# Expert MLP on one core: the first x tile loaded in two halves with different packet sizes, and the b2 load moved behind the entry of the main block

## The chip, the cores and the metric

The kernel runs on one core of one Trainium2 chip. The metric is the device time of one execution in microseconds. The core has a matrix engine (PE, whose weight loads are listed apart as PEld), a vector engine (DVE), a scalar engine (ACT), a general engine (POOL, written `nc.gpsimd` in the code) and a synchronising engine (SP, `nc.sync`). Sixteen DMA engines carry all transfers between the main memory and the core's on-chip memory. Loads that POOL issues run on the queue that the profile calls q0 (software_dynamic), those that SP issues on q1 (hardware_dynamic).

## What is computed

There are 8 experts. Each has 256 tokens, a hidden size of 512 and an inner size of 2048. All arrays arrive as 32-bit floats.

```python
h = np.maximum(np.matmul(x, w1) + b1[:, np.newaxis, :], 0)   # x 8x256x512, w1 8x512x2048
out = np.matmul(h, w2) + b2[:, np.newaxis, :]                # w2 8x2048x512
```

The weights are 8 x 4 MiB for `w1` and as much for `w2`; x and the output have 4 MiB each.

## The kernel before, in words

**Layers.** The inner size is cut into `nJ` = 16 columns of 128. For one expert, layer 1 (L288) makes 64 matmuls: 16 columns by 4 slices of the hidden size. The weights `w1sb` are the stationary operand and the turned input `xTsb` streams past them. ACT applies bias and relu to each column (L106) and writes `hTsb` in 16 bits. Layer 2 starts with the bias `b2` as a one-row matmul (L303) and adds 32 matmuls (L318), two token blocks by 16. ACT, and for the last two experts also DVE, carry the results out of the accumulators (L118). One loop on PE (L268) runs E + LAG = 11 steps: layer 1 of expert `step`, and from step 3 on layer 2 of expert `step - 3`.

**Loads of weights.** POOL issues them all (`run_gpsimd`, L157). `w1sb` and `w2sb` have three slots each. The load also converts from 32 to 16 bits, so a 4 MiB expert becomes 2048 KB. The order on q0 is written out by hand: `w1` of experts 0, 1 and 2 as early as possible, then, in step 3, `w1` of expert 3, `w2` of expert 0; x of experts 4 to 7 in step 4, and so on in turn. `w1` of expert e from 3 on waits until layer 1 of expert e - 3 is done (L162); `w2` waits in the same way for layer 2 (L167). At the end POOL and SP issue the output transfers (L187, L155, L389).

**The beginning, outside the main block.** `first_loads` (L340) issues on SP, in this order: x of expert 0 into `pair0`, x of expert 1 into `pair1` (512 KB each, 128 rows of 4 KB), the `b1` rows (64 KB), and x of experts 2 and 3 into `outg` (1024 KB, 128 rows of 8 KB). On POOL it issues `w1` of expert 0 and `b2` (8 KB when converted). `first_turns` (L354) builds an identity matrix (POOL zeroes `steps`, DVE turns it at L360, ACT copies four blocks at L363), casts x of experts 0 and 1 (ACT, L365), turns them with 16 matmuls against the identity (PE, L372), copies the result to `xTsb` (ACT, L373), and turns the `b1` rows with four DVE transposes (L375). The order of the instructions of these two functions on each engine is chosen by a scheduler, except for loads that `keep_in_program_order` fixes.

**The entry.** The rest runs inside a block (L381) whose order and semaphores are written by hand. ACT, DVE, PE and SP enter it only after everything ahead of it that it depends on is done: every load of `first_loads` has landed, and all of `first_turns` has run. POOL alone enters at once, issues `w1` of experts 1 and 2, and makes up for the wait later (L180). Within the block ACT first casts x of experts 2 and 3 (L195), and DVE turns it (L222).

**Semaphores near the change.** The arrival of `w1` of expert e counts on `s_w1[e % 3]`, 16 per load. SP waits for it at L144 and raises `w1_in`, for which PE waits (L271). Slot 1 is used by experts 1, 4 and 7.

Of the kernel before, what the change touches and what calls it, by code (L numbers as in the profile page):

```python
# [10 lines left out]
def kernel(  # L11
# [9 lines left out]
    nc = tc.nc  # L21
# [3 lines left out]
    E, T, H = x.shape  # L25
    M = w1.shape[2]
    P = 128
# [4 lines left out]
    nB = P // B  # L32
    LAG = 3
    NW = 3
# [13 lines left out]
    def sb(name, shape, dt=fp16):  # L48
        return nc.alloc_sbuf_tensor(name, shape, dt).ap()

    w1_f = sb("w1sb", [P, NW * nKC * M + nJ])
    w1_sb = w1_f[:, 0 : NW * nKC * M].rearrange("p (n kc m) -> p n kc m", n=NW, kc=nKC)
# [6 lines left out]
    b2_sb = sb("b2sb", [1, E * H])  # L59
    b1_rows = sb("b1rows", [E * nB, M // nB], fp32)  # L60
# [9 lines left out]
    def sem(name):  # L70
        return nc.alloc_semaphore(name)

    s_x = sem("s_x")
    s_w1 = [sem(f"s_w1_{i}") for i in range(NW)]
# [51 lines left out]
    def out_of(first, n):  # L126
        return out[first : first + n].rearrange("e (p r) h -> (e p) r h", r=n * nTB)

    x32 = {e: pair[e] for e in range(2)}
    x32[2] = grouped[0][:, 0 : FIRST[2] * nTB, :]  # L130

    def w1_of(e):
        return w1[e].rearrange("(p kc) m -> p kc m", kc=nKC)

    def x_of(first):
        n = FIRST[first]
        return x[first : first + n].rearrange("e (p r) h -> (e p) r h", r=n * nTB)

    def run_sync():
        s = nc.sync  # L140
        for step in range(E + LAG):
            if step < E:
                if step:
                    s.wait_ge(s_w1[step % NW], 16 * ((step + NW - 1) // NW))  # L144
                s.sem_inc(w1_in, 1)  # L145
            if step >= LAG:
                e = step - LAG
                for h in range(2):
                    if (e, h) in s_w2:
                        s.wait_ge(s_w2[e, h], 16)  # L150
                    s.sem_inc(w2_in, nQ // 2)  # L151
                    if e == E - 1 and h == 0:
                        s.wait_ge(po_free_a, E)
                        s.wait_ge(po_free_d, E)
                        s.dma_start(out=out_of(E - 2, 1), in_=pair[0]).then_inc(s_out[E - 2], 16)  # L155

    def run_gpsimd():  # L157
        g = nc.gpsimd

        def load_w1(e):  # L160
            if e >= NW:
                g.wait_ge(ph_full, nJ * (e - NW + 1))  # L162
            g.dma_start(out=w1_sb[:, e % NW], in_=w1_of(e)).then_inc(s_w1[e % NW], 16)  # L163

        def load_w2(e):
            if e >= NW:
                g.wait_ge(po_full, ENDS * (e - NW + 1))  # L167
            src = w2[e].rearrange("(p j) h -> p j h", j=nJ)
            cuts = (0, CUT[e], nJ) if e in CUT else (0, nJ)
            for h, (lo, hi) in enumerate(zip(cuts, cuts[1:])):  # L170
                g.dma_start(  # L171
                    out=w2_sb[:, e % NW, lo:hi], in_=src[:, lo:hi]).then_inc(s_w2[e, h], 16)

        for step in range(1, E + LAG):
            if step < E:
                if step == 4:
                    g.dma_start(out=x16[step], in_=x_of(step)).then_inc(s_x, 16)
                load_w1(step)
            if step == NW - 1:
                tc.wait_critical_data_deps()  # L180
            if step >= LAG:
                load_w2(step - LAG)
        g.wait_ge(s_w2[E - 1, 0], 16)
        for first in sorted(GROUPS, reverse=True):
            done = 1 + first + GROUPS[first]
            g.wait_ge(po_free_a, done)
            g.dma_start(out=out_of(first, GROUPS[first]), in_=grouped[first]).then_inc(  # L187
                s_out[first], 16)
# [149 lines left out]
                t.wait_ge(ph_free, turned)  # L338

    def first_loads():  # L340
        for to, rows in (
            (x32[0], x_of(0)),
            (x32[1], x_of(1)),
            (b1_rows, b1.rearrange("e (b i) -> (e b) i", b=nB)),
            (x32[2], x_of(2)),
        ):
            tc.keep_in_program_order(nc.sync.dma_start(out=to, in_=rows))  # L347
        for to, rows in (
            (w1_sb[:, 0], w1_of(0)),
            (b2_sb, b2.rearrange("e h -> (e h)").rearrange("(o f) -> o f", o=1)),  # L350
        ):
            tc.keep_in_program_order(nc.gpsimd.dma_start(out=to, in_=rows))

    def first_turns():  # L354
        g, v, a, t = nc.gpsimd, nc.vector, nc.scalar, nc.tensor
# [18 lines left out]
        for b in range(nB):  # L374
            v.transpose(  # L375
                out=b1T[b * B : (b + 1) * B, nB - 1 - b : nB - 1 - b + nJ * B],
                in_=b1_rows.rearrange("r (i j) -> r j i", j=nJ))

    first_loads()
    first_turns()  # L380
    with tc.tile_critical(sync_engine=mybir.EngineType.Pool, no_gpsimd_drain=True):  # L381
        run_gpsimd()
        run_sync()
        run_scalar()
        run_vector()
        run_tensor()
        nc.sync.wait_ge(po_free_a, 1 + E)
        nc.sync.wait_ge(po_free_d, 1 + E)
# [38 lines left out]
```

## Time and profile before

| | |
|---|---|
| median of three runs | 180.65 us (180.57 to 181.31) |
| the profiled execution's own time | 180.67 us |
| its span, first to last instruction | 178.9 us |
| mean granted TensorE clock | 0.969 |
| PE busy | 130.8 us, 73% of the span |
| ACT busy | 86.2 us, 48% |
| DVE busy | 37.7 us, 21% |
| POOL busy | 13.4 us, 7% |
| DMA packets and bytes | 3825 packets, 40.98 MB |
| share of the 16 DMA engines' span, q0 and q1 | 95.2% and 4.5% |

The span is measured by the hardware profiler from the first to the last instruction; the execution's own time has 1.8 us more around it. A row of the timeline gives start, duration, engine, line, operation and operands, and in brackets how long the engine sat idle before it and what ended that. The DMA view can be asked for any stretch of the span: it then counts the packets of each queue whose start falls into it, and a strip of 40 digits gives the busy share of the 16 engines in 40 equal slices of the stretch, in tenths. A row of its list of issues has the bytes of one load and the time from issue to landing.

The page counts 448 packets under 512 bytes and 28 loads and stores: 16 of these short packets to each, one for every DMA engine. They close a transfer and are called closing packets below.

### The profile page before, as it was taken

Reading aid. Unit: us, or ns where it says so; the run is one execution under the profiler, and the core shown is the slowest. Engines: PE = TensorE matmul, PEld = TensorE weight load, DVE = VectorE, ACT = ScalarE, POOL = GpSimd, SP = SyncE. Lnnn points to the kernel's source line nnn. Section 1 sums busy time; section 2 is a strip of 40 time slices with the busy share of each in tenths; the row PEclk is TensorE's granted clock in tenths of the full one; section 3 lists DMA queues with packets and bytes.
Section 4 is the critical chain, followed back from the end, with each engine's and each line's share of the span. In section 5 each row is a group of like instructions: output and inputs, shape, how many; then the busy total and the mean of one; then the engine's idle time right before and its main releaser. Section 6 shows DMA issues by size and latency. Waiting matters only on the chain.

```text
span 178.9 us, 2880 instructions
## 1 busy us (share of the span) xinstructions
PE 130.8 (73%) x800; PEld 87.1 (49%) x800; DVE 37.7 (21%) x39; ACT 86.2 (48%) x160; POOL 13.4 (7%) x30
## 2 busy tenths in 40 slices
PE   0002299596969996999949993899389997997950
PEld 0002178585858742794338642764178543442410
DVE  0074099500000299992000000000000000001010
ACT  3302847585877803892099408970578303131010
POOL 7100000302020001001000001000200002000200
PEclk9999999999999999699999999999969999999995
DMA  5999989999999999998999999999899899999996
GB/s 215 265 255 277 233 183 231 234 205 207 234 209 202 234 212 198 234 231 183 231 234 201 209 234 205 205 234 220 191 234 231 187 227 205 214 213 212 335 440 256
DMA packets 3825, 40.98 MB, mean 229 GB/s; under 512 B 448, under 2 KB 464, under 8 KB 1136
## 3 DMA queue, kind: packets, MB, share of 16 engines
q0 software_dynamic: 3056, 37.76, 95.2%
q1 hardware_dynamic: 768, 3.21, 4.5%
q14 instruction: 1, 0.01, 0.0%
HBM read 71.39 MB, written 4.19 MB: 422 GB/s over the span
## 4 chain that ended last, share of the span: by engine, by line
DMA 62%; PE 20%; DVE 6%; ACT 4%; issue 3%; SPq 1%; ACTq 0%
DMA w1sb<-in_w_dram 43%; PE ph L288 12%; DMA outg<-in_x_dram 10%; DMA w2sb<-in_w_dram 10%; PE po L318 8%; DVE xTsb L222 6%; ACT hTsb L106 3%; ACT x L195 1%; SPq L347 1%; PE po L303 0%; ACT pair L118 0%; ACTq L422 0%; SPq L145 0%; SPq L151 0%; ACTq L194 0%
## 5 line engine op out<-in xcount | busy, mean ns | idle before, releaser
L288 PE MATMUL ph<-xTsb,w1sb 128*128 x512 | 68.1, 293 | 21.7 <-SPq L145 10.4
L288 PEld LDWEIGHTS ph<-xTsb,w1sb 128*128 x512 | 59.0, 148 | 31.9 <-issue 29.0
L106 ACT ACTIVATE hTsb<-ph,b1T 128x256 f16<-128x256 f32 x128 | 56.8, 474 | 15.4 <-PE ph L288 14.9
L318 PE MATMUL po<-w2sb,hTsb 128*128 x256 | 56.6, 379 | 2.3 <-SPq L151 2.3
L118 ACT COPY outg<-po 32x1024 f32<-32x1024 f32 (+1 forms) x20 | 20.1, 1005 | 43.3 <-PE po L318 43.2
L318 PEld LDWEIGHTS po<-w2sb,hTsb 128*128 x256 | 25.0, 98 | 32.8 <-issue 5.0
L222 DVE STREAM_TRANSPOSE xTsb<-x 32x512 f16<-32x512 f16 (+1 forms) x32 | 31.0, 970 | 35.0 <-DMA x<-in_x_dram 27.7
L118 DVE COPY pair<-po 128x512 f32<-128x512 f32 x2 | 1.4, 691 | 88.4 <-PE po L318 88.4
L372 PE MATMUL ph<-ident,x 128*128 128x128 f16 x16 | 1.9, 313 | 16.6 <-ACT ident L363 16.6
L171 POOL DMA_DIRECT2D w2sb<-in_w_dram x10 | 5.3, 534 | 70.7 <-PE po L318 70.7
L372 PEld LDWEIGHTS <-x 128*128 128x128 f16 x16 | 1.6, 148 | 16.6 <-ACT ident L363 16.6
L163 POOL DMA_DIRECT2D w1sb<-in_w_dram x7 | 3.7, 535 | 64.6 <-PE ph L288 64.4
L118 ACT COPY pair<-po 128x512 f32<-128x512 f32 x2 | 1.2, 585 | 13.8 <-PE po L318 13.8
L375 DVE STREAM_TRANSPOSE b1T<-b1rows 32x512 f32<-32x512 f32 x4 | 4.1, 1023 | 10.2 <-DMA b1rows<-in_b_dram 10.1
L303 PE MATMUL po<-b2sb,ones 1*128 x16 | 4.8, 379 | 0.9 <-issue 0.7
L363 ACT COPY ident<-hTsb 32x32 f16<-32x32 f16 x4 | 1.0, 240 | 9.2 <-DVE hTsb L360 9.1
L365 ACT CAST x<-pair 128x1024 f16<-128x1024 f32 x2 | 2.1, 1044 | 2.3 <-DMA pair<-in_x_dram 2.3
L303 PEld LDWEIGHTS po<-b2sb,ones 1*128 1x128 f16 x16 | 1.4, 91 | 3.5 <-issue 3.3
L373 ACT COPY xTsb<-ph 128x1024 f16<-128x1024 f16 x2 | 1.9, 1015 | 1.1 <-PE ph L372 1.1
L187 POOL DMA_DIRECT2D out_dram<-outg x2 | 1.1, 536 | 16.7 <-DMA w2sb<-in_w_dram 16.7
L195 ACT CAST x<-outg 128x2048 f16<-128x2048 f32 x1 | 1.9, 1900 | 0.8 <-DMA outg<-in_x_dram 0.8
L365 ACT ACT_TABLE_LOAD x1 | 1.3, 1283 | 0.7 <-PEq L411 0.7
(12 smaller groups left out, 5.0 us busy)
## 6 DMA issues: line engine op xcount, KB each, us to landing
w1sb<-in_w_dram POOLq DMA_DIRECT2D x8, 2048.0 KB, 30.6
w2sb<-in_w_dram POOLq DMA_DIRECT2D x6, 2048.0 KB, 43.8
w2sb<-in_w_dram POOLq DMA_DIRECT2D x2, 1024.0 KB, 28.4
out_dram<-outg POOLq DMA_DIRECT2D x1, 2048.0 KB, 10.9
w2sb<-in_w_dram POOLq DMA_DIRECT2D x1, 1408.0 KB, 17.5
pair<-in_x_dram SPq DMA_DIRECT2D x2, 512.0 KB, 3.8
outg<-in_x_dram SPq DMA_DIRECT2D x1, 1024.0 KB, 17.8
x<-in_x_dram POOLq DMA_DIRECT2D x1, 1024.0 KB, 27.7
```

Of the source, the lines that this page charges most:

```text
L106: return nc.scalar.activation(out=to, in_=columns, func=relu_of, bias=b1T[:, at : at + 1], scale=1.0)
L118: return copy(out=t.rearrange("p (tb s) h -> p tb s h", s=split)[at : at + rows, lo:hi, k, :], in_=po[k * rows : (k + 1) * rows, e % 2, lo ...
L163: g.dma_start(out=w1_sb[:, e % NW], in_=w1_of(e)).then_inc(s_w1[e % NW], 16)
L171: g.dma_start(out=w2_sb[:, e % NW, lo:hi], in_=src[:, lo:hi]).then_inc(s_w2[e, h], 16)
L195: a.copy(out=x16[2], in_=x32[2]).then_inc(cast, 1)
L222: ins = v.transpose(out=to[b * B : (b + 1) * B, :, :, half * B : (half + 1) * B], in_=src.rearrange("p r (i kc) -> p kc r i", kc=nKC))
L288: ins = t.matmul(out=ph[i][:, 0:T], lhsT=w1_cols(w1_j, i, kc), rhs=x_cols[kc], start=(kc == 0), stop=(kc == nKC - 1),)
L303: t.matmul(out=po_f[:, bass.ds(o + tb * 512, H)], lhsT=ones1, rhs=b2_sb[0:1, bass.ds(b_e, H)], start=True, stop=False, skip_group_check=True,)
L318: ins = t.matmul(out=po_f[:, bass.ds(o + tb * 512, H)], lhsT=hT_f[:, bass.ds(h_e + (j * T + tb * P), P)], rhs=w2_f[:, bass.ds(w_e + j * H, ...
L365: a.copy(out=x16[e], in_=x32[e])
L372: t.transpose(out=to[:, kc, r, :], in_=rows[:, kc, :], identity=ident)
L375: v.transpose(out=b1T[b * B : (b + 1) * B, nB - 1 - b : nB - 1 - b + nJ * B], in_=b1_rows.rearrange("r (i j) -> r j i", j=nJ))
```

## The change

Three things are edited.

1. x of expert 0 is loaded by two instructions in place of one: partitions 0 to 63 cut into packets of 2 KB (`max_dma_last_dim` of 4 * 512 bytes), partitions 64 to 127 in rows of 4 KB as before. SP therefore issues five loads in place of four, and x of expert 1, the `b1` rows and x of experts 2 and 3 come one place later in its order.
2. The `b2` load leaves `first_loads`. POOL issues it as its first instruction inside the block, ahead of `w1` of expert 1.
3. It counts on the semaphore of slot 1, and SP waits there for 16 more.

```diff
             if step < E:
                 if step:
-                    s.wait_ge(s_w1[step % NW], 16 * ((step + NW - 1) // NW))
+                    s.wait_ge(s_w1[step % NW], 16 * ((step + NW - 1) // NW + (step % NW == 1)))
...
+        g.dma_start(
+            out=b2_sb, in_=b2.rearrange("e h -> (e h)").rearrange("(o f) -> o f", o=1),
+        ).then_inc(s_w1[1], 16)
         for step in range(1, E + LAG):
...
     def first_loads():
-        for to, rows in (
-            (x32[0], x_of(0)),
-            (x32[1], x_of(1)),
-            (b1_rows, b1.rearrange("e (b i) -> (e b) i", b=nB)),
-            (x32[2], x_of(2)),
+        half = P // 2
+        for to, rows, packet in (
+            (x32[0][:half], x_of(0)[:half], 4 * H),
+            (x32[0][half:], x_of(0)[half:], None),
+            (x32[1], x_of(1), None),
+            (b1_rows, b1.rearrange("e (b i) -> (e b) i", b=nB), None),
+            (x32[2], x_of(2), None),
         ):
-            tc.keep_in_program_order(nc.sync.dma_start(out=to, in_=rows))
-        for to, rows in (
-            (w1_sb[:, 0], w1_of(0)),
-            (b2_sb, b2.rearrange("e h -> (e h)").rearrange("(o f) -> o f", o=1)),
-        ):
-            tc.keep_in_program_order(nc.gpsimd.dma_start(out=to, in_=rows))
+            tc.keep_in_program_order(nc.sync.dma_start(
+                out=to, in_=rows, max_dma_last_dim=packet))
+        tc.keep_in_program_order(nc.gpsimd.dma_start(out=w1_sb[:, 0], in_=w1_of(0)))
```

Two moves follow from it that the diff does not show; they come from the scheduler. On DVE the transposes ran as `b1` four times (L375), then the identity's (L360); in the changed kernel they run as `b1` once, the identity's, `b1` three times. And ACT's loading of its function table, which waited for nothing, now waits for the second half of x of expert 0.

## The prediction

> **What bounds the kernel now.** I read the page's DMA strip first, then the busy times by stage, then the beginning on SP, POOL and in the DMA view.
>
> ```profile
> DMA  5999989999999999998999999999899899999996
> ```
>
> ```profile
> 37.50:147.00 109.50, 92.35 (x593) 64.05 (x591) 19.78 (x16) 63.27 (x123) 5.82 (x11) 0.97 1.02 217
> ```
>
> The first strip says that after the first slice of 4.5 us the sixteen DMA engines are never less than eight tenths busy. In the second row (a stage of 109.5 us; PE, PEld, DVE, ACT and POOL busy, clock, DMA share, GB/s) the DMA share is 1.02 while PE is busy for 92 of 109.5 us. The kernel is bound by the weight stream. A change in front of it matters only if it adds bytes or packets, or lets the stream run dry. One 2048 KB load is 2.097 MB, at 217 GB/s 9.66 us; 128 packets of 16 KB are 8 for each engine, 1.21 us each.
>
> The beginning is where the change is. SP's issues, one row from the chain of waits, and POOL's:
>
> ```profile
> 0.74 0.86 SPq L347 DMA_DIRECT2D pair<-in_x_dram  x2
> 1.65 0.42 SPq L347 DMA_DIRECT2D b1rows<-in_b_dram  x1
> 2.12 0.42 SPq L347 DMA_DIRECT2D outg<-in_x_dram  x1
> ```
>
> ```profile
> 1.18 0.42 SPq L347
> ...
> 2.12 17.78 DMA outg<-in_x_dram
> ```
>
> ```profile
> 1.25 0.67 POOL L352 DMA_DIRECT2D w1sb<-in_w_dram  x1 [0.81 <-POOLq L411]
> 1.91 0.51 POOL L352 DMA_DIRECT2D b2sb<-in_b_dram  x1
> ...
> 3.97 1.09 POOL L163 DMA_DIRECT2D w1sb<-in_w_dram  x2 [0.16 <-issue]
> 32.75 0.53 POOL L163 DMA_DIRECT2D w1sb<-in_w_dram  x1 [27.69 <-PE ph L288]
> ```
>
> SP issues x0 at 0.74, x1 at 1.18, b1 at 1.65, x2 (experts 2 and 3) at 2.12. POOL issues w1 of expert 0 at 1.25, **between x1 and b1**. The DMA view of two stretches, 1.5 to 4.6 and 4.6 to 5.9 us, shows what the engines made of that:
>
> ```profile
> DMA  0000395269477969699899999999969696979898
> ...
> q1 hardware_dynamic: 262, 1.01, 84.6%
> ```
>
> ```profile
> q0 software_dynamic: 16, 0.26, 99.1%
> q1 hardware_dynamic: 26, 0.04, 8.4%
> ```
>
> Up to 4.6 only SP's packets run; the first starts in the fifth slice of 0.0775 us, at 1.81, 1.07 after its issue. Then come 26 more of SP's and exactly one w1 packet for each engine. 262 + 26 = 288 is all of x0 and x1, (8 data + 1 closing) x 2 x 16. So on every engine both x loads ran to their end, and then w1 came ahead of b1, though b1 had been issued 0.3 us before POOL's instruction for w1 was over and, at SP's 1.07, was there by 2.72. After that the two queues take turns (rows further down). I read this as first come, first run: an engine works off packets in the order in which they were handed to it, one from each queue in turn once both have work. w1 was handed over after x1 (1.18 + 1.07 = 2.25) and before b1 (2.72), that is 1.00 to 1.47 us after its own issue at 1.25.
>
> The end of the span supports it. The last store is issued here, and the stretches 174.4 to 175.9 and 175.9 to 178.9 show:
>
> ```profile
> 173.28 0.34 SPq L389 DMA_DIRECT2D out_dram<-pair  x1
> ```
>
> ```profile
> q0 software_dynamic: 38, 0.62, 96.7%
> ```
>
> ```profile
> q1 hardware_dynamic: 144, 0.52, 42.7%
> q0 software_dynamic: 16, 0.00, 0.3%
> ```
>
> With 1.07 us it was there at 174.35, yet q0 ran 38 more packets of 16 KB, and SP's 144 came only when q0 had its closing packets left. It did not cut in.
>
> **What the entry waits for.** The chain row above has x2 issued at 2.12 and landed at 19.90; ACT and PE follow:
>
> ```profile
> 15.58 1.00 ACT L363 COPY ident<-hTsb 32x32 f16<-32x32 f16 x4 [9.15 <-DVE hTsb L360]
> 17.71 1.93 ACT L373 COPY xTsb<-ph 128x1024 f16<-128x1024 f16 x2 [1.14 <-PE ph L372]
> 20.44 1.90 ACT L195 CAST x<-outg 128x2048 f16<-128x2048 f32 x1 [0.80 <-DMA outg<-in_x_dram]
> ```
>
> ```profile
> 22.05 10.40 PE L288 MATMUL ph<-xTsb,w1sb 128*128 x64 [3.52 <-issue]
> 34.25 8.09 PE L288 MATMUL ph<-xTsb,w1sb 128*128 x64 [1.79 <-DVE xTsb L222]
> ```
>
> The turned x is done at 17.71 + 1.93 = 19.64, x2 at 19.90; so x2 opens the block, PE works from 22.05 to 32.45, and only then can POOL issue w1 of expert 3 (32.75). The stretch 36.0 to 37.0 and the list of issues show when that load ran:
>
> ```profile
> DMA  0000000000000000000099999000990999900900
> ```
>
> ```profile
> w1sb<-in_w_dram POOLq DMA_DIRECT2D x1, 2048.0 KB, 14.2
> ```
>
> The next packets start at 36.5 (21st slice of 0.025); the load lands at 32.75 + 14.2 = 46.95, 10.4 after 36.5, one load's 9.66 and a little. So w1 of expert 2 ended and w1 of expert 3 began at 36.5. It was handed over at 32.75 + 1.00 to 1.47 = 33.75 to 34.22: the entry may be **2.3 to 2.7 us later before the stream runs dry**.
>
> **The change part by part.**
>
> *x1 one place later.* x0 becomes two loads, at 0.74 and 1.18; x1 goes out at 1.65, b1 at 2.12, x2 near 2.57. x1 stands where b1 stood, and b1 at 1.65 came behind w1 on all sixteen engines. So x0 runs alone, and x1's nine packets per engine alternate with w1's. Behind the first w1 packet SP's queue then has 9 (x1) + 3 (b1) + 9 (x2) = 21 packets per engine instead of 12, and before the last of them 21 of POOL's have run: 9 of w1 of expert 0, 2 of b2, 9 of w1 of expert 1, 1 of w1 of expert 2, with 8 + 8 + 1 = 17 of 16 KB. Before, 12 held 9 + 2 + 1, with 9. Eight more are 8 x 1.21 = 9.66 us.
>
> *Packets of 2 KB.* The stretch 5.9 to 7.2 us holds one packet of each queue per engine, SP's being b1's rows of 2 KB:
>
> ```profile
> q0 software_dynamic: 16, 0.26, 96.9%
> q1 hardware_dynamic: 16, 0.03, 7.3%
> ```
>
> 7.3% of 1.3 us is 0.095 us for one packet of 2 KB; the 262 packets above (246 of 4 KB, 16 closing) filled 84.6% of 3.1 us on 16 engines, 0.17 us for one of 4 KB. x0 becomes 8 short and 4 long ones per engine: 8 x 0.095 + 4 x 0.17 - 8 x 0.17 = **+0.1 us**. The bounds are 0 (bytes alone) and +0.7 (a short one as dear as a long one); I take the first figure, since its row is of the same size and queue.
>
> *b2.* POOL's order on q0 stays w1 of expert 0, b2, w1 of experts 1 and 2. b2's 0.51 us of issue move behind the memsets, so w1 of expert 1 still goes out at 3.97. b2 landed here:
>
> ```profile
> b2sb<-in_b_dram POOLq DMA_DIRECT2D x1, 8.0 KB, 15.7
> ```
>
> At 1.91 + 15.7 = 17.6 it was ahead of 19.90, so the entry gains nothing; the w1 load ahead of it hides its later issue by over 10 us. SP's longer wait counts b2 with the load behind it in the same queue: nothing. Behind that wait SP has only the signals for later weights.
>
> *DVE's and ACT's order.* DVE's rows:
>
> ```profile
> 10.14 4.13 DVE L375 STREAM_TRANSPOSE b1T<-b1rows 32x512 f32<-32x512 f32 x4 [10.14 <-DMA b1rows<-in_b_dram]
> 14.30 1.25 DVE L360 STREAM_TRANSPOSE hTsb<-hTsb 128x1024 f16<-128x1024 f16 x1
> ```
>
> b1 will land behind 9 w1 packets instead of 3, at 10.14 + 6 x 1.21 + 0.1 = 17.5. One b1 transpose (4.13 / 4 = 1.03) and the identity's (1.25) end at 19.8; from the identity's copies to the turned x it took from 15.58 to 19.64, 4.06, so 23.9. x1 stands ahead of b1 in SP's queue, so its cast is over by then, and ACT's table load waits only for x0, which runs alone. All of it lies beside x2's load: the 3.1 us by which the reorder brings the identity forward are worth nothing while x2 is last. If x2 landed as early as now, they would still leave x2 last.
>
> *The sum.* x2 lands at 19.90 + 9.66 + 0.1 = 29.7; PE starts at 31.8, w1 of expert 3 is issued at 32.75 + 9.76 = 42.5 and handed over at 43.5 to 44.0, middle 43.75. The stream runs dry at 36.6 and resumes there: 43.75 - 36.5 = **+7.25 us**. Behind that PE is 9.8 late and the stream 7.25. Waits for a weight load absorb the difference:
>
> ```profile
> 72.00 9.23 PE L288 MATMUL ph<-xTsb,w1sb 128*128 x64 [2.19 <-SPq L145]
> ```
>
> ```profile
> 130.15 9.39 PE L288 MATMUL ph<-xTsb,w1sb 128*128 x64 [3.15 <-SPq L145]
> ```
>
> Of each, about 1.8 is the gap that PE has anyway (the row at 34.25, whose w1 had landed); the rest, 0.4 at 72.00 and 1.35 at 130.15 with two expert steps between, is room for most of the 2.6, and what is left of it the loads issued long ahead hide. With the profiled execution's 180.67 (its span 178.9 and 1.8 around it; the median of the runs, 180.65, is the same) that is **187.9 us**; by the ends of the handover 187.7 to 188.2, and with the packets' upper bound (+0.7) on one side and as much on the other for a quicker restart 187.0 to 188.7. PE's 10.40 us for expert 0 are taken as they are: it comes to that work from a wait now as then.
>
> **A rule weighed.** The stretch 10.5 to 15.5, three turns of an engine, in which x2 runs beside w1:
>
> ```profile
> q0 software_dynamic: 48, 0.79, 73.6%
> q1 hardware_dynamic: 48, 0.39, 19.3%
> ```
>
> Three packets of each queue per engine: they alternate one by one, and the sum uses that. The Trainium skill, "DMA: Bandwidth & Descriptors", section "Queues, rings and completion order", says that an engine takes turns between queues but drains some 9 to 17 descriptors of one before it switches. By that rule whole loads would alternate; this trace disagrees, 48 against 48, and the rule keeps a small chance as the third rival.
>
> **The rivals.**
>
> *x1 stays ahead of w1 (not slower).* It decides when POOL's packets are handed over: if later than 2.72, more than 1.47 us after their issue, or if x1 is ready faster than b1 was, the order is as before. Then x2 lands 0.1 later, inside the room of 2.3 us, and the time is 180.67 + 0.1 = 180.8. For it: between the two places lie only 0.47 us, and what the trace shows is one execution. Against it: all sixteen engines had w1 ahead of b1, and x1 takes just b1's place with four times b1's packets. The same time results if w1 was merely not ready before 4.6 by chance, and each engine then alternates: one or two packets of x1 remain, 1.2 to 2.4 us, inside the room or at its edge. Against that: no engine broke into x1, though they end x1 at different times. The Trainium skill, in the same page's "Specifications", puts the first byte at about 0.6 us on SP's path and about 1 us on POOL's; by these x1 and w1 would both be there at 2.25, a tie that leaves the time open between 180.8 and 187.9. The trace has 1.07 for SP's first packet and b1 behind w1, and speaks against it. Chance 0.12.
>
> *A part of x1 gets ahead.* Each of its packets that does saves 1.21 us. With four of nine ahead, five are left: 5 x 1.21 - 2.5 of room + 0.1, 184.3. Chance 0.04, spread over 181 to 187.
>
> *Whole loads alternate.* Then x2 has 16 packets of w1 ahead of it, not 17: 187.9 - 1.2 = 186.7. Chance 0.03, by the 48 against 48.
>
> *x0's second half falls behind w1 too.* It goes out at 1.18, x1's place, whose margin to w1 the trace does not give. Its five packets would cost 5 x 1.21 = 6.1 more: 194.0. Against it: it has half of x1's packets, and x1 got through whole. Chance 0.04.
>
> If the rows were not cut to 2 KB after all, the fifth load would still be there, and the forecast stands.
>
> **How the numbers follow.** Forecast 187.9 with 0.77; x1 ahead 0.12; a part ahead 0.04; whole loads 0.03; x0's half behind 0.04. From 184.0 to 189.0 lie the forecast, the whole loads and half of the partial case: 0.82. Those at 180.8 and 194.0 are left out. About 0.5% (0.9 us) is what a measurement of this kernel can tell from no change: slower by more has 0.87, within it 0.12 (x1 ahead), faster 0.01, for which I see no mechanism, since no byte is saved and no gap closed.
>
> **What would show it.** In the DMA view of the changed kernel, the stretch up to about 3.5 us should hold some 220 packets of SP's (x0's two halves) and then one w1 packet per engine, with x1 behind it; w1's first packet comes near 3.4 instead of 4.6. x1 should land near 15, b1 near 17.5, x2 near 29.7. DVE should show the identity's transpose as its second. PE should begin layer 1 near 31.8, POOL issue w1 of expert 3 near 42.5, and the DMA strip have a hole of some 7 us from about 36.6. If x1 lands before the first w1 packet starts and x2 near 20, the first rival holds. If x2 is late but the strip has no hole, I misjudged the room; if the hole is there and the end is not later, something behind it gave the time back, which the full strip excludes in my reading.

## The result, and the profile after

The kernel with the change takes **195.6 us** (median of six runs, 194.94 to 196.71); the kernel before, on the same chip, 180.66 (180.57 to 181.31). The ratio is 1.082, with a 95% interval from 1.079 to 1.086. The profiled execution took 195.66 us, its span 193.9, at a granted clock of 0.966 (before 0.969): 14.99 us more than the profiled execution of before. The forecast was 187.9, its range 184.0 to 189.0. The direction and the place are as forecast, the size is twice as large. Ratios here and below leave out executions that were more than 1.5% slower than the fastest of their kernel; medians and ranges have all of them.

The DMA strip of the page of the changed kernel, in 40 slices of 4.85 us, and the row of a stretch that I set from 36.50 to 50.55 us (columns as in the prediction: PE, PEld, DVE, ACT and POOL busy, clock, DMA share, GB/s):

```profile
DMA  6999999500699999999999999999999999999996
```

```profile
36.50:50.55 14.05, 10.01 (x64) 8.30 (x64) 11.08 (x16) 9.21 (x17) 1.22 (x3) 1.00 0.00 0
```

The DMA view of the same stretch has only w1 of expert 2's closing packets:

```profile
q0 software_dynamic: 16, 0.00, 0.2%
```

The hole that the prediction looked for is there. Counted as the prediction counts it, from 36.5 to the first packet of w1 of expert 3, it is not 7.25 us long but 14.05. In that whole stretch no packet with data starts, while PE computes layer 1 of expert 0 and DVE and ACT turn x2. (A view puts a packet where it starts. The last data packets of w1 of expert 2 start just before 36.5 and take 1.2 us each, so the engines stand empty from about 37.5.) Everywhere else the strip is as full as before.

What the entry waited for, in the chain of waits from the start on (start, duration, what), with ACT's and PE's rows and POOL's next weight load from the timeline:

```profile
0.74 0.73 SPq L352
...
1.53 0.58 SPq L352
...
2.16 0.58 SPq L352
...
2.78 0.44 SPq L352
...
3.27 33.51 DMA outg<-in_x_dram
```

```profile
37.31 1.90 ACT L198 CAST x<-outg 128x2048 f16<-128x2048 f32 x1 [6.46 <-DMA outg<-in_x_dram]
38.92 10.12 PE L291 MATMUL ph<-xTsb,w1sb 128*128 x64 [9.18 <-SPq L145]
49.33 0.53 POOL L163 DMA_DIRECT2D w1sb<-in_w_dram  x1 [44.23 <-PE ph L291]
```

As before it is x2 that opens the block: it lands at 3.27 + 33.51 = 36.78, PE starts at 38.92, and w1 of expert 3 can go out at 49.33. The SP rows show something else as well: the issue of x0's first half took 0.73 us, that of its second half 0.58 and that of x1 0.58, where the two x loads of before went out 0.44 apart. So x0's second half went out at 1.53, **behind** POOL's w1 of expert 0:

```profile
1.25 0.67 POOL L354 DMA_DIRECT2D w1sb<-in_w_dram  x1 [0.80 <-POOLq L413]
```

SP's first packet is late too: it starts at 2.25, 1.51 after its issue, where the prediction had read 1.07 from the kernel before (strip of the stretch 1.5 to 4.0, slices of 0.0625 us):

```profile
DMA  0000000000009724995008968998999909000000
```

The packets of each queue, of three stretches in the DMA view of the changed kernel, 1.5 to 4.0, 3.55 to 5.0 and 5.0 to 6.5 us:

```profile
q0 software_dynamic: 16, 0.26, 56.4%
q1 hardware_dynamic: 144, 0.26, 42.3%
```

```profile
q0 software_dynamic: 16, 0.26, 86.9%
q1 hardware_dynamic: 1, 0.00, 0.1%
```

```profile
q0 software_dynamic: 17, 0.28, 87.2%
q1 hardware_dynamic: 16, 0.07, 12.6%
```

144 packets are 128 of 2 KB and 16 closing ones: the first half of x0 and nothing else. Then comes one w1 packet per engine, then a second one with none of SP's between them, and only in the third stretch does x0's second half begin, one packet in turn with each of w1's.

The arithmetic of the end, in the prediction's own steps:

| step | before | after | difference |
|---|---|---|---|
| x2 lands | 19.90 | 36.78 | +16.88 |
| PE starts layer 1 | 22.05 | 38.92 | +16.87 |
| w1 of expert 3 issued | 32.75 | 49.33 | +16.58 |
| its first packet | 36.5 | 50.55 | +14.05 |
| it lands | 46.95 | 61.83 | +14.88 |
| the execution's own time | 180.67 | 195.66 | +14.99 |

The last load landed 12.5 us after its issue by the list of issues (49.33 + 12.5 = 61.83):

```profile
w1sb<-in_w_dram POOLq DMA_DIRECT2D x1, 2048.0 KB, 12.5
```

From the fourth row to the fifth the hole costs 0.8 us more than its length: from its first packet to its landing this load took 11.28 us, where the same load took 10.45 in the full stream of before. The DMA view from 50.55 to 51.7 us shows where a part of that lies:

```profile
q0 software_dynamic: 16, 0.26, 155.6%
```

These are the first packets of the sixteen engines. 155.6% of 1.15 us is 1.79 us for each, against the prediction's 1.21 in the full stream.

### The profile page after: what moved, and what is told of

Its sections match the earlier page's. It is cut to its first block, busy times and chain, and to the rows that moved or that the text cites. A ratio compares the mean times of both kernels' runs of the same rounds, so it can differ in the third digit from the quotient of the medians.

```text
span 193.9 us, 2882 instructions
## 1 busy us (share of the span) xinstructions
PE 131.4 (68%) x800; PEld 87.6 (45%) x800; DVE 37.7 (19%) x39; ACT 86.2 (44%) x160; POOL 13.4 (7%) x30
## 4 chain that ended last, share of the span: by engine, by line
PE 49%; ACT 21%; DMA 17%; DVE 6%; issue 3%; SPq 1%; ACTq 0%
PE po L321 29%; PE ph L291 18%; DMA outg<-in_x_dram 17%; ACT hTsb L106 11%; ACT outg L118 8%; DVE xTsb L225 6%; PE po L306 2%; SPq L352 1%; ACT x L198 1%; ACT pair L118 0%; ACTq L424 0%; ACTq L197 0%; ACTq L196 0%; ACTq L195 0%; ACTq L194 0%
## 5 line engine op out<-in xcount | busy, mean ns | idle before, releaser
L291 PE MATMUL ph<-xTsb,w1sb 128*128 x512 | 68.8, 296 | 28.0 <-ACT hTsb L106 10.5
L291 PEld LDWEIGHTS ph<-xTsb,w1sb 128*128 x512 | 59.6, 148 | 38.3 <-issue 34.6
L118 ACT COPY pair<-po 128x512 f32<-128x512 f32 x2 | 1.2, 585 | 12.5 <-PE po L321 12.5
L367 ACT ACT_TABLE_LOAD x1 | 1.3, 1283 | 12.2 <-DMA pair<-in_x_dram 12.2
L375 ACT COPY xTsb<-ph 128x1024 f16<-128x1024 f16 x2 | 1.9, 1015 | 1.1 <-PE ph L374 1.1
```

The lines of the kernel that those rows point to most:

```text
L118: return copy(out=t.rearrange("p (tb s) h -> p tb s h", s=split)[at : at + rows, lo:hi, k, :], in_=po[k * rows : (k + 1) * rows, e % 2, lo ...
L291: ins = t.matmul(out=ph[i][:, 0:T], lhsT=w1_cols(w1_j, i, kc), rhs=x_cols[kc], start=(kc == 0), stop=(kc == nKC - 1),)
L367: a.copy(out=x16[e], in_=x32[e])
```

## The experiments

Two explanations stood against each other at first. One: the split alone moves x0's second half behind w1 of expert 0, because SP issues it too late, and each own packet that x2 then has ahead of it costs 1.21 us; the late entry lets the stream run dry. The rivals: the short packets, the b2 edit or the new order on DVE cost something too; and, called theory D in the expectations, the stream is not what sets the end any more, but PE and ACT, which come to their work so late. A later question (theory F) was why SP's issues had become longer.

### One part of the change at a time

`e1_b2_only` is the kernel before with the b2 edit alone:

```diff
-            (b2_sb, b2.rearrange("e h -> (e h)").rearrange("(o f) -> o f", o=1)),
...
+        g.dma_start(out=b2_sb, in_=...).then_inc(s_w1[1], 16)
         for step in range(1, E + LAG):
```

> Theory A (order): the time is lost because x of expert 0's second half, x of expert 1, b1 and x of experts 2 and 3 are handed to the DMA engines after w1 of expert 0; with the b2 edit alone SP's loads are as before, so the time is that of before, 180.7 us within 0.5, with x2 landed near 19.9. Rival B (b2): b2's new place and the longer wait on slot 1 cost the time; then near 195.6. Rival C (packets): the cut of x0 into smaller and more packets costs it; then also 180.7.

`e2_split_only` is the kernel before with the two loads of x0 alone:

```diff
-            (x32[0], x_of(0)),
+            (x32[0][:half], x_of(0)[:half], 4 * H),
+            (x32[0][half:], x_of(0)[half:], None),
```

> Theory A: the split alone brings the whole loss, 195.6 us within 0.7, x2 landed near 36.8. Rival B: 180.7. Rival C: 195.6 as well.

| kernel | us (runs) | ratio to before | 95% interval |
|---|---|---|---|
| `e1_b2_only` | 180.74 (180.53 to 181.53) | 1.000 | 0.9985 to 1.002 |
| `e2_split_only` | 195.53 (195.12 to 195.82) | 1.080 | 1.076 to 1.083 |

The split is the whole loss, and the b2 edit costs nothing and gains nothing. With b2 alone x2 lands where it did (chain of waits of `e1_b2_only`):

```profile
2.12 17.80 DMA outg<-in_x_dram
```

In `e2_split_only` DVE keeps the order of before, b1 four times and then the identity, and PE still starts at 38.94 (changed kernel: 38.92). So the new order on DVE is worth nothing, as forecast. ACT's table load waits for x0's second half in this kernel too (it starts at 12.29, in the changed kernel at 12.22), so the two do not price that move; in both it is over more than 20 us before x2 lands.

### Packet size, or number and shape of the loads

`e4_halves_both_4k` keeps the two halves and leaves the first one uncut; `e5_one_load_2k` keeps one load and cuts it to 2 KB (the rest as before).

```diff
-            (x32[0][:half], x_of(0)[:half], 4 * H),
+            (x32[0][:half], x_of(0)[:half], None),
```

> The changed kernel with both halves of x0 in rows of 4 KB. Theory A, if the cut to 2 KB is what made SP's first issue 0.73 us long: the issues stand at 0.74, 1.18 and 1.65, x0 is whole ahead of w1, x1 behind it, x2 lands near 30 and the time is 187 to 190. Theory A, if every load of 64 rows is slow to issue: 195.6. Rival C: no short packets, so 180.7 to 181.5.

```diff
-            tc.keep_in_program_order(nc.sync.dma_start(out=to, in_=rows))
+            tc.keep_in_program_order(nc.sync.dma_start(
+                out=to, in_=rows, max_dma_last_dim=4 * H if to is x32[0] else None))
```

> The kernel before with x of expert 0 still one load of 128 rows, but cut to packets of 2 KB; b2 as before. In the run with both halves in 4 KB rows SP's first issue took 0.56 us, with the 2 KB cut 0.73, in the kernel before 0.39. Theory A (order decides): if the cut makes the issue longer by those 0.17 us, x of expert 1 goes out near 1.35 and the ninth packet of x1 is at the margin to w1 (2.25 to 2.7): either x1 stays ahead, 180.7 to 182, or it falls behind w1, x2 lands near 30 and the time is 188 to 190.5. Rival C (short packets cost by themselves): x0 has twice the packets of the changed kernel's first half, so 195 or more whatever the order in the DMA view.

`e4_halves_both_4k`: 195.15 us (194.74 to 195.79), ratio 1.079 (1.075 to 1.084), the loss of the full change. `e5_one_load_2k`: median of ten runs 180.97, ratio 1.0005 (0.9992 to 1.0018) over eight of them, no loss. (The other two took 186.1 and 186.9. No trace shows why; SP's second load, x1, goes out at 1.24 there, practically together with w1 at 1.25.) So the cut to 2 KB is free in those eight, and two half loads cost the whole 15 us. The chains of waits, `e4_halves_both_4k` first:

```profile
0.74 0.56 SPq L352
...
1.35 0.57 SPq L352
...
1.98 0.58 SPq L352
...
2.60 0.43 SPq L352
...
3.08 32.65 DMA outg<-in_x_dram
```

```profile
0.74 0.44 SPq L347
...
1.24 0.45 SPq L347
...
1.74 0.42 SPq L347
```

One load of 128 partitions goes out in 0.44 us even when it is cut; a load of 64 partitions takes 0.56 and 0.57 without any cut, and so does x1 behind it.

Are two loads then slow in themselves? `e11_column_halves` splits x0 by columns: two loads of all 128 partitions, 2 KB per row each.

```diff
-            (x32[0][:half], x_of(0)[:half], 4 * H),
-            (x32[0][half:], x_of(0)[half:], None),
+            (x32[0][:, 0:1], x_of(0)[:, 0:1], None),
+            (x32[0][:, 1:2], x_of(0)[:, 1:2], None),
```

> The changed kernel with x0 split by columns: two loads of 128 rows of 2 KB in place of two of 64 rows. Theory F (loads of 64 rows are slow to issue, and so is the load behind them): all issues take about 0.42 us, at 0.74, 1.18, 1.65, 2.12, 2.57. Then x0 is whole ahead of w1 and x1 behind it, the case that the prediction forecast: x2 lands near 30, w1 of expert 3 goes out near 42.8, and the time is 187.9 by the prediction's sum, 189 to 190 with what PE and ACT add. Rival G (any fifth load slows SP's issues): issues of 0.55, x0's second part behind w1, 194.5 to 196.

190.77 us (189.53 to 191.2), ratio 1.052 (1.048 to 1.056). Its chain of waits, and its packets from 1.5 to 4.6 and from 4.6 to 6.0 us:

```profile
0.74 0.39 SPq L351
...
1.18 0.42 SPq L351
...
1.65 0.42 SPq L351
...
2.12 0.43 SPq L351
...
2.60 29.37 DMA outg<-in_x_dram
```

```profile
q1 hardware_dynamic: 288, 0.52, 50.1%
q0 software_dynamic: 12, 0.20, 44.5%
```

```profile
q0 software_dynamic: 15, 0.25, 100.8%
q1 hardware_dynamic: 7, 0.03, 5.4%
```

These are, to the hundredth, the issue times that the prediction gave the changed kernel (0.74, 1.18, 1.65, 2.12). With them x0 runs whole ahead of w1: 288 packets are both halves, 144 each. So it is loads of 64 partitions that go out slowly; that there are five loads instead of four does not do it. x2 lands at 2.60 + 29.37 = 31.97 and not at 29.7. The last fence shows part of why: up to 6.0 us 27 w1 packets have started and only 7 of x1's, so at least four w1 packets ran as a second one, with none of x1's between.

### Where w1 of expert 0 stands

The other side of the race: the split stays, and POOL issues w1 later. `e3_split_w1_behind_memsets` puts that load behind POOL's four memsets; `e8_w1_behind_x1` and `e13_w1_far_behind` repeat one of the memsets, two and three times in all.

```diff
-        tc.keep_in_program_order(nc.gpsimd.dma_start(out=w1_sb[:, 0], in_=w1_of(0)))
...
+        g.memset(steps, 0.0)
...
+        tc.keep_in_program_order(nc.gpsimd.dma_start(out=w1_sb[:, 0], in_=w1_of(0)))
```

> The changed kernel with POOL's first w1 load issued behind its four memsets, near 2.6 us instead of 1.25. Theory A: both halves of x0 and x1 (issued up to 2.16) are then handed over ahead of w1, x2 lands near 16 to 21 and the time is back at 180.7 to 182, although the split is as in the changed kernel. Rival C: the split costs what it costs, 195 or more. Rival B: 195 or more.

> The changed kernel with w1 of expert 0 issued still later on POOL, behind the four memsets with one of them done twice (near 2.9 us). Theory A: x1, issued at 2.16, is handed over near 3.2 and w1 near 3.9 or later, so all of x0 and x1 and perhaps b1 and a part of x2 run ahead of w1; x2 lands near 20 or earlier, inside the room, and the time is 180.5 to 181.7 with the split left in. Rival C: 189 or more, since the split is in it.

> The changed kernel with w1 of expert 0 issued behind the memsets with one of them done three times (near 3.8 us). Theory A: w1 is handed over after x1 on all engines, x2 lands at 20 or earlier and the time is 180.7 to 181.7, in every run, with the split left in. Rival C: over 186, since the split is in it.

The first three columns of figures are from the profiled execution of each kernel.

| kernel | w1 (expert 0) issued | x2 lands | w1 (expert 3) issued | us (runs) |
|---|---|---|---|---|
| the changed kernel | 1.25 | 36.78 | 49.33 | 195.6 |
| `e3_split_w1_behind_memsets` | 1.98 | 30.63 | 43.29 | 189.99 (189.11 to 190.82) |
| `e8_w1_behind_x1` | 2.87 | 29.90 | 42.43 | 186.3 (183.47 to 188.64) |
| `e13_w1_far_behind` | 3.88 | 14.9 | 31.80 | 182.96 (182.53 to 183.25) |

The ratios are 1.050 (1.045 to 1.056) for the second row and 1.012 (1.009 to 1.014) for the last; the four runs of the third lie too far apart for one (183.47, 185.04, 187.56, 188.64). With the same two half loads in place, one later w1 takes the 15 us loss back to 2.0 (182.96 against 180.97 of before in the same series). That settles the direction: it is the order of w1 and x, not the halves' bytes or packets.

The first step did not give what I expected of it. I had taken w1 to go out behind x1; POOL began the memsets earlier, so w1 went out at 1.98, between x0's second half (1.53) and x1 (2.16):

```profile
1.98 0.67 POOL L361 DMA_DIRECT2D w1sb<-in_w_dram  x1
```

By chance that is the case which the prediction took for the changed kernel: x0 whole ahead of w1, x1 behind it (from 1.5 to 6.0 us the DMA view counts 224 packets of SP's, all of x0, and 16 of w1; from 6.0 to 7.2 there are 16 of each). It gave 190, not 187.9: x2 lands at 30.63, 0.9 later than the forecast's 29.7.

The third missed too. w1 went out 0.71 us behind x1 and should have left x1 alone. The trace is of the slowest execution, the one of 188.64 us. Its packets from 1.5 to 5.4 and from 5.4 to 6.8 us:

```profile
q1 hardware_dynamic: 276, 0.74, 74.5%
q0 software_dynamic: 1, 0.02, 2.6%
```

```profile
q0 software_dynamic: 15, 0.25, 100.0%
q1 hardware_dynamic: 58, 0.15, 28.1%
```

x0 and x1 together are 368 packets here (144 + 80 + 144), x0 alone 224. By 6.8 us 334 of SP's have started while 16 of w1 have. Had every engine put w1 ahead of x1, two of x1's per engine at most could have run beside these, 224 + 32 = 256 in all; had every engine run x1 first, x1 would have landed here. But the list of issues has it at 2.16 + 15.1 = 17.3:

```profile
pair<-in_x_dram SPq DMA_DIRECT2D x1, 512.0 KB, 15.1
```

So **some engines ran x1 first and others put w1 ahead of it**. The trace also has the arrival of each engine's share of x1: eight land from 6.3 to 7.2 us, the other eight from 11.7 to 17.3. The race is decided engine by engine, and a load has landed only when the last of the sixteen has done its share; so x2 lands almost as late (29.90) as in `e3_split_w1_behind_memsets`, where w1 was ahead on all of them. The spread of the four runs would fit that, but only one of them has a trace.

In the fourth, x2 lands early, and the entry waits for w1 of expert 0 instead (chain of waits of `e13_w1_far_behind`; the list of issues has x2 at 11.6 us, so 3.25 + 11.6 = 14.9):

```profile
3.88 15.76 DMA w1sb<-in_w_dram
```

```profile
22.16 9.34 PE L291 MATMUL ph<-xTsb,w1sb 128*128 x64 [12.56 <-issue]
```

PE starts as in before (22.05). The remaining 2.0 us go with the start of the stream: in the first 4.53 us the engines move 123 GB/s, in before 216 (row of that stretch in each kernel, before first):

```profile
0.00:4.53 4.53, 0.00 (x0) 0.00 (x0) 0.00 (x0) 1.64 (x2) 3.31 (x12) 1.00 0.56 216
```

```profile
0.00:4.53 4.53, 0.00 (x0) 0.00 (x0) 0.45 (x1) 1.28 (x1) 3.93 (x11) 1.00 0.50 123
```

(216 - 123) GB/s x 4.53 us are 0.42 MB, at the stream's 217 GB/s 1.9 us. The stream keeps that delay: w1 of expert 3, though issued 0.95 earlier than in before, lands at 31.80 + 17.0 = 48.80, 1.85 later, and the profiled execution is 1.86 longer than that of before.

```profile
w1sb<-in_w_dram POOLq DMA_DIRECT2D x1, 2048.0 KB, 17.0
```

`e10_x1_first_halves_4k` goes at the same order from SP's side: x1 first, then the two halves of x0, uncut.

```diff
-            (x32[0][:half], x_of(0)[:half], 4 * H),
-            (x32[0][half:], x_of(0)[half:], None),
             (x32[1], x_of(1), None),
+            (x32[0][:half], x_of(0)[:half], None),
+            (x32[0][half:], x_of(0)[half:], None),
```

> The kernel with both halves of x0 in 4 KB rows, but with x1 issued ahead of them. Theory A: x1 goes out at 0.74 and the first half near 1.18, both ahead of w1; the second half (near 1.8) falls behind it with b1 and x2. Behind the first w1 packet SP has 5 + 3 + 9 = 17 packets per engine, 14 of 16 KB run before the last of them, 5 more than before: x2 lands near 26 and the time is 184 to 187. If issues of 64 rows are the slow ones, x1's takes 0.4 us here and the halves 0.56; if the first three are slow whatever they are, x1's takes 0.56 too and both halves may fall behind, x2 near 32, 191 to 192. Rival C: 195, as with the halves in the other order.

188.59 us (187.76 to 190.09), ratio 1.043 (1.038 to 1.047), above what I expected. Chain of waits:

```profile
0.74 0.38 SPq L352
...
1.18 0.53 SPq L352
...
1.77 0.58 SPq L352
...
2.39 0.58 SPq L352
...
3.02 28.35 DMA outg<-in_x_dram
```

x1, now ahead of the half loads, goes out in 0.38 us; the halves take 0.53 and 0.58, and b1 behind them 0.58. Slow, then, are the loads of 64 partitions and the one right behind them; x2's own issue, the second behind them, takes 0.95 here, which is not explained. The second half of x0 goes out at 1.77 and falls behind w1. The first half goes out at 1.18, ahead of w1's 1.25, and still does not get through whole: its shares land on ten engines by 5.5 us and on the other six from 7.1 to 12.2. Before, x1 as one load of 128 partitions, issued at the same 1.18, had landed by 5.4. So a half load loses time after its issue as well. x2 lands at 31.37, where 26 was expected.

`e14_before_w1_behind_memsets` asks whether before itself gains if w1 and b2 give way: both stand behind the memsets.

```diff
-        for to, rows in ((w1_sb[:, 0], w1_of(0)), (b2_sb, ...)):
-            tc.keep_in_program_order(nc.gpsimd.dma_start(out=to, in_=rows))
         g.memset(steps, 0.0)
+        for to, rows in ((w1_sb[:, 0], w1_of(0)), (b2_sb, ...)):
+            tc.keep_in_program_order(nc.gpsimd.dma_start(out=to, in_=rows))
```

> The kernel before with w1 of expert 0 and b2 issued behind the memsets (w1 near 2.0 instead of 1.25). Theory A with the stream as the bound: x0, x1 and b1 run ahead of w1 on every engine, x2 lands at or before 19.9, the entry is 1 to 4 us earlier, and the time stays at 180.7 within 0.4, because the stream is full either way: an earlier entry is worth nothing. Rival H (the entry sets the time in both directions): 177 to 180.

181.93 us (181.42 to 182.13), ratio 1.004 (1.002 to 1.007). x2 lands at 18.9, 1.0 earlier, but b2 then ends the wait (2.64 + 16.67 = 19.31, chain of waits), and PE starts at 21.89 in place of 22.05:

```profile
2.64 16.67 DMA b2sb<-in_b_dram
```

The expectation of 180.7 within 0.4 missed: the kernel is 1.0 us slower than before (180.97 in the same series), a small loss, but its interval leaves out 1. w1 of expert 3 goes out 1.02 us earlier than in before, at 31.73, and lands later, at 31.73 + 16.3 = 48.03 instead of 46.95:

```profile
w1sb<-in_w_dram POOLq DMA_DIRECT2D x1, 2048.0 KB, 16.3
```

So an earlier entry bought nothing where the stream does not run dry. The stream itself ran 1.1 us behind, which fits the later issue of w1 of expert 0, at 1.98. No version here beats the kernel before.

### Is it still the stream that sets the end?

Behind the hole, the rows of PE in the changed kernel name ACT and no longer a weight load:

```profile
91.47 7.15 PE L291 MATMUL ph<-xTsb,w1sb 128*128 x48 [2.63 <-ACT hTsb L106]
```

Theory D reads that as the new bound. `e6_dve_evicts_on_after` therefore lets DVE evict half of every expert's layer 2, which takes work from ACT; `e7_dve_evicts_on_e3` does the same on `e3_split_w1_behind_memsets`.

```diff
-        return 0 if e in GROUP_OF else nTB // 2
+        return nTB // 2
```

> The changed kernel with DVE carrying half of every expert's results out of the accumulators (the same edit as in the 190.4 run, whose entry came 2 us later by itself and hid the effect). Here x0's second half is firmly behind w1, so the entry stays near 36.8. Theory D (after a late entry PE and ACT set the pace): PE's stalls for ACT of 2.6 us per expert shrink below 1, waits for weights come back, and the time falls from 195.6 to what the restart of the stream allows, 180.67 + (50.55 - 36.5) = 194.7, within 0.5. Rival E (the restart of the stream sets all of the loss): 195.6.

> The kernel of the run in which w1 is issued behind the memsets (190.0 us), with DVE carrying half of every expert's results out of the accumulators, where ACT carried all of the first six. Theory D (after a late entry PE and ACT, not the weight stream, set the pace: PE stalls 2.4 to 2.7 us per expert for ACT): the stalls shrink, PE waits for weights again, and the time falls to what the late restart of the stream allows, 180.67 + (44.5 - 36.5) = 188.7, within 0.4. Rival E (the stream or its late restart sets everything that is lost): 190.0 as before the edit.

`e6_dve_evicts_on_after`: 195.37 us (195.05 to 195.6), within the spread of the changed kernel's runs. The forecasts of D and E are only 0.9 us apart and the median lies between them, so the time alone does not decide. The waits for ACT give way to waits for weights:

```profile
106.14 6.07 PE L292 MATMUL ph<-xTsb,w1sb 128*128 x48 [2.62 <-SPq L145]
```

With ACT relieved, PE runs into the stream at once. What decides is the landing of w1 of expert 3. In this kernel it comes at 49.21 + 12.5 = 61.71, 14.76 later than in before, and the profiled execution (195.6) is 14.93 longer; in the changed kernel the two are 14.88 and 14.99. So PE and ACT hold no more than some 0.2 us of the loss; the rest of the 0.9 us that theory D gives them lies ahead of that landing, in the hole's end. Theory D falls.

`e7_dve_evicts_on_e3` gave 190.44 (189.27 to 193.58) against 189.99; by its time alone it is inconclusive, since x2 landed at 32.73 in it, 2.1 later than in the kernel it was made from, before any eviction. But here too the loss is that of the landing: 45.35 + 12.7 = 58.05 is 11.10 later than in before, the profiled execution (191.82) 11.15 longer. The two figures agree within 0.25 us in `e1_b2_only`, `e3_split_w1_behind_memsets`, `e5_one_load_2k`, `e10_x1_first_halves_4k`, `e13_w1_far_behind` and `e14_before_w1_behind_memsets` as well. In `e2_split_only`, `e4_halves_both_4k` and `e11_column_halves` the execution is 0.6, 1.0 and 0.9 us longer than the landing accounts for; what adds that is open.

## Why the prediction was wrong, point by point

**Right.** The bound: the weight stream, and one later entry that lets it run dry near 36.5. The room ahead of that: 2.3 to 2.7 forecast, 16.58 - 14.05 = 2.53 measured. Of the rule that an engine takes packets in the order in which they were handed over, then one of each queue in turn, the second half: 16 against 17 from 5.0 to 6.5 us. The first half holds only in part. The 144 packets above fit it, but its handover times, 1.07 us after SP's issue and 1.00 to 1.47 after POOL's, are not those of every load: SP's first packet came after 1.51 us here, and in `e8_w1_behind_x1` they would have put x1 (2.16 + 1.07) ahead of w1 (2.87 + 1.00) on every engine, where on eight w1 got ahead of much or all of it. The whole-load rival, which took the Trainium skill's "DMA: Bandwidth & Descriptors" ("Queues, rings and completion order") at its word, is out: from 5.0 to 6.5 us the queues alternate one by one. b2, worth nothing: `e1_b2_only`. The packets of 2 KB, +0.1: `e5_one_load_2k`, 1.0005. DVE's order, worth nothing: `e2_split_only`. The identity's transpose is DVE's second, as announced.

**The step that failed** is the first of the change: "x0 becomes two loads, at 0.74 and 1.18; x1 goes out at 1.65, b1 at 2.12, x2 near 2.57", and with it "So x0 runs alone". I took the issue time of a load of 128 partitions (0.39 to 0.42) for one of 64. Measured: 0.73 and 0.58. x0's second half left at 1.53, not 1.18, on the other side of POOL's 1.25. `e11_column_halves` shows the step itself to be right in its consequence for loads of 128 partitions: with issue times as I gave them, x0 does run alone. For a half load even 1.18 would have been at the edge: the one that went out then in `e10_x1_first_halves_4k` fell at least in part behind w1 on six engines. The case that came was in the list, "x0's second half falls behind w1 too", priced 194.0, with a chance of 0.04 and "it has half of x1's packets, and x1 got through whole" against it. That reason looked at how many packets there are; what decided was when they were issued.

**The sum by packets.** Behind the first half of x0, SP's queue now holds 5 (second half) + 9 + 3 + 9 = 26 packets per engine; with the extra w1 packet of the stretch 3.55 to 5.0, 27 of POOL's run before the last of them: 9 of expert 0, 2 of b2, 9 of expert 1 and 7 of expert 2. Of 16 KB are 8 + 8 + 7 = 23, where before had 9: 14 x 1.21 = 16.9, and x2 landed 16.88 later. That it fits so closely is partly luck. The sum leaves out that w1's first packets start near 3.3 us instead of 4.6, and that twelve packets of 4 KB per engine, by the prediction's 0.17 us 2.0 in all, now lie behind them; the two nearly cancel. The forecast had 17 of them; the second half behind w1 adds five, the extra packet one. From there: 16.88 becomes 16.58 at the issue; less the room of 2.53 that is the hole's 14.05; with 0.8 at its end it is 14.9.

**The hole's end** is the other term that was missed. I had the load resume as it ran before, or up to 0.7 quicker; it took 0.8 more from first packet to landing. The other kernels with a hole repeat it: 12.4 to 12.7 us from the issue of this load to its landing. `e3_split_w1_behind_memsets`, the forecast's own case, shows what the forecast would have lacked without the failed step: x2 0.9 later than 29.7 (not explained) and a hole's end as above, together 190.0 in place of 187.9.

**Open.** Why a load of 64 partitions takes SP 0.53 to 0.73 us where b1's 32 partitions take 0.42 to 0.47, and why the next load is slow too, and why half loads also start later after their issue: the runs show that it is so, not why. Also open is what lets a second w1 packet ahead in the changed kernel and on some engines of `e11_column_halves`, while in before every engine took b1 after the first.

## What to carry to other kernels

Where two queues feed the same engines, a small load's cost is its place in the order: here, once both queues had work, every packet of x that came behind the first of w1 waited for one 16 KB packet, 1.21 us, and a first half load that took a third of a microsecond longer to issue than a load of 128 partitions helped to cost some 5 us (195.6 against 190.77 of `e11_column_halves`). Before splitting or adding a load at the start, list the issue times of all queues, and take the duration of each issue from a load of the same shape; where none is in the trace, price the case in which it falls behind. A stream that bounds the kernel forgives an early or a late entry until its queue is empty; find that point first (2.5 us away here), since beyond it each microsecond counts in full.

## What the runs showed of the hardware

- SP needs 0.38 to 0.47 us to issue a load of 128 partitions or of b1's 32 rows, 0.53 to 0.73 for one of 64 partitions, and 0.58 for the load right behind such a one (`e4_halves_both_4k`, `e10_x1_first_halves_4k`); one issue, x2's in `e10_x1_first_halves_4k`, took 0.95. The cut to 2 KB adds little to a load of 128 (0.44, `e5_one_load_2k`); the longest of the halves, 0.73, is the one that is cut.
- SP's first packet starts 1.07 us after the issue when the first load has 128 partitions (before), 1.51 when it has 64 (the changed kernel).
- The order of two queues is decided by each of the sixteen engines for itself: with w1 issued 0.71 us behind x1 (`e8_w1_behind_x1`) eight engines had x1 through by 7.2 us, the other eight only from 11.7 to 17.3, with w1's packets between.
- A stream that has run dry costs more than the pause: 11.28 us from first packet to landing for 2048 KB, against 10.45 in the full stream; the first packet on each engine takes 1.79 us on average, against 1.21.
- A stream that bounds the kernel keeps a late start: in `e13_w1_far_behind` 1.85 us at the landing of w1 of expert 3 and 1.86 at the end.
